# Loads and first groups in arrival order, a staged norm chain, and w_o tiles moved among the ff1 groups of a hybrid decoder block

## The chip, the cores and the metric

One Trainium2 chip, 8 cores, each with its own slice of the batch and sequence and no traffic between them. The metric is device time in microseconds of the slowest core, as the median of several executions. TensorE (PE in the profile) multiplies and transposes; VectorE (DVE), ScalarE (ACT) and GpSimd (POOL) do the elementwise work and SyncE (SP) issues loads and stores.

Some executions fall in a slow state, in which the cores of a die show a lower granted clock (in the slow run of start_only, 1174.41 us, 0.859 to 0.866 on one die against 0.965 to 0.967 on the other). The time after "Measured" is the median of all executions; those of wgp_only, start_only, staged_in_place and stage_c_last take in one slow run each, that of tr5_first two.

## The reference, cut to what matters

```python
u = rms_norm(h, mix_pre_g)
proj = u @ w_in                       # GLU (2 x 1024), pool (1024), gates (2 x 1024)
y_conv = conformer_conv_branch(...)   # GLU, depthwise conv of 31, layer norm, swish, projection
y_pool = pooling_branch(...)          # trailing means, per-group linear, projection
merged = g_conv * y_conv + g_pool * y_pool
h = h + rms_norm(merged @ w_o, mix_post_g)
v = rms_norm(h, mlp_pre_g)
v = jnp.square(jax.nn.relu(v @ w_ff1)) @ w_ff2
h = h + rms_norm(v, mlp_post_g)
```

A core has 2048 positions: 16 tiles of 128, in 4 blocks of 512. Products are in bf16, norms in float32.

## The kernel before: the parts that matter

All instructions are recorded in one order, and each engine carries out its own in that order. A helper adds the semaphore waits, so a late producer holds everything that is recorded behind its consumer on the same engine. The stages are: pool projection (`p_group`), GLU with the convolution, two gated stages, w_o with the first ff1 block, then ff2 and three more ff1/ff2 blocks.

```python
def x_norm(j):                                   # ACT square+sqrt, DVE reciprocal and scaling
    r = rstd(src, P, 0, dst, "act")
    STT(dst, src, r, gb0[:P, :], ALU.mult, ALU.mult)      # L250
def x_tr(j):                                     # 8 transposes (L223), one copy, ACT or DVE in turn
    ...
for blk in range(4):                             # projection
    if blk == 0:
        p_halo()                                 # first, and needs all of the weights
    for cc in range(8):
        nxt = 4 * (blk + 1) + cc // 2
        if cc % 2 == 0 and nxt < 16: x_norm(nxt)
        p_group(cc, blk)
        if cc % 2 == 1 and nxt < 16: x_tr(nxt)
        ...
# (cut: GLU, convolution; gated stages)
wload2(wgp, w_in_v[:, :, 4096:5120])             # after the GLU loop
def wo_tile(j):
    ...                                          # 16 matmuls
    resid(b, gb1, 2, res, dst[:, 0:512], j, "pool")   # 2 squares, add, POOL rsqrt, 4 DVE steps
    r = rstd(res, 128, 0, dst, "pool")                # square, POOL rsqrt
    STT(dst, res, r, gb2, ALU.mult, ALU.mult)         # second norm
for blk in range(4):                             # second gated stage
    for cc in range(8):
        gated(cc, blk, wco, s_t, wgc, False)
        if blk and cc % 2 == 1: wo_step()        # 12 of the 16 tiles here
        elif blk and len(trq) > 1: h_tr(trq.popleft())
# (cut: the other 4 tiles stand among the first 8 of the 32 ff1 groups of block 0)
FF1_ORDER = (0, 4, 1, 5, 2, 6, 3, 7)             # order in which ff2 takes its weight chunks
```

## Time and profile before

| | kernel before |
|---|---|
| first runs | 1085.21, 1088.69 (fast), 1103.85, 1107.53 (slow) |
| profiled span | 1084.3 us, fast, core 2 |
| PE busy | 972.8 us |
| projection ends (first GLU matmul) | 120.1 us |
| GLU stage | 154.0 |
| wait for `wgp` and first gated stage | 154.7 |
| second gated stage | 153.8 |
| ff1 of block 0, to the start of ff2 | 103.4 |
| the rest | 398.3 |

The rows from "projection ends" on add up to the span, and each is the time between two marks on PE. What a change does is looked for in the row where it acts. The lines of the profile are in the prediction.

### The profile page before, as it was taken

What the parts mean: (1) busy time and instruction counts of PE and PEld (TensorE: products, weight loads), DVE (VectorE), ACT (ScalarE), POOL (GpSimd) and SP (SyncE); (2) the same over time, 40 slices, a digit from 0 to 9 for tenths busy, and PEclk for the clock granted to TensorE, in tenths of its full rate; (3) what the DMA queues carried; (4) which work ended last, traced back from release to release, by engine and by line L of the source; (5) the groups of instructions that cost most, each with busy time, mean ns of one, the idle gap of its engine ahead of it and who ended that gap; (6) DMA issues with size and microseconds to landing.
All of it is one profiled execution on the core that took longest, in us unless ns stands there. A gap on an engine that the chain in (4) does not pass through costs nothing.

```text
span 1084.3 us, 14235 instructions; the slowest of 8 cores (1072.2 to 1084.3 us)
## 1 busy us (share of the span) xinstructions
PE 972.8 (90%) x5042; PEld 488.0 (45%) x5136; DVE 424.6 (39%) x685; ACT 311.9 (29%) x565; POOL 62.6 (6%) x112
## 2 busy tenths in 40 slices
PE   1578999999199999999999679899999999999997
PEld 1333557666054454444444334344444444444443
DVE  2276662344025412356565444124422342234222
ACT  3355213234021344133433343112321232123210
POOL 2000000100000000011211130000000000000000
PEclk9998999999689999999999979999999999999999
DMA  9922534993858002242837579522002200220021
GB/s 186 192 97 55 104 40 99 128 167 59 135 99 155 1 1 78 31 112 91 175 97 177 124 154 161 105 78 78 1 1 78 78 0 2 78 77 2 1 70 66
DMA packets 49748, 93.03 MB, mean 86 GB/s; under 512 B 6640, under 2 KB 29424, under 8 KB 48528
## 3 DMA queue, kind: packets, MB, share of 16 engines
q0 software_dynamic: 32416, 46.14, 27.8%
q1 hardware_dynamic: 17264, 45.99, 12.8%
q8 instruction: 42, 0.69, 0.3%
q14 instruction: 26, 0.21, 0.1%
HBM read 121.42 MB, written 16.84 MB: 128 GB/s over the span
## 4 chain that ended last, share of the span: by engine, by line
PE 75%; DMA 9%; DVE 6%; issue 4%; ACT 3%; POOL 1%; DVEq 0%; ACTq 0%; SPq 0%; POOLq 0%
PE ps L220 72%; DMA arena<-w_in 5%; DMA arena<-w_ff 4%; ACT arena L238 3%; PE ps L223 2%; DVE arena L250 2%; DVE arena L241 2%; DVE arena L436 1%; DVE ps L250 1%; DMA arena<-xh 1%; POOL arena L262 1%; POOL sm L370 1%; DVE ps L246 0%; DVE arena L256 0%; POOL sm L369 0%
## 5 line engine op out<-in xcount | busy, mean ns | idle before, releaser
L220 PE MATMUL ps<-arena 128*128 128x512 bf16 (+2 forms) x4514 | 941.2, 367 | 57.1 <-DMA arena<-w_in 33.8
L220 PEld LDWEIGHTS ps<-arena 128*128 128x128 bf16 x4608 | 453.8, 104 | 525.9 <-issue 81.8
L238 ACT ACTIVATE arena<-ps 128x512 bf16<-128x512 f32 (+5 forms) x382 | 237.4, 638 | 655.6 <-PE ps L220 469.5
L246 DVE TENSOR_SCALAR ps<-ps 128x512 f32<-128x512 f32 x128 | 88.2, 698 | 108.4 <-PE ps L220 108.4
L241 DVE TENSOR_TENSOR arena<-ps,arena 128x512 f32<-128x512 f32 (+3 forms) x116 | 87.0, 755 | 92.9 <-ACT arena L238 61.8
L250 DVE SCALAR_TENSOR_TENSOR arena<-arena,ps 128x512 bf16<-128x512 f32 (+1 forms) x64 | 43.9, 685 | 127.5 <-ACT arena L238 72.1
L223 PE MATMUL ps<-identb,arena 128*128 128x128 bf16 (+1 forms) x520 | 40.4, 230 | 46.4 <-DVE arena L250 29.4
L241 DVE TENSOR_TENSOR sm<-sm 128x1 f32<-128x1 f32 x32 | 5.0, 157 | 191.9 <-ACT arena L238 191.9
L223 PEld LDWEIGHTS ps<-identb,arena 128*128 128x128 bf16 (+1 forms) x520 | 34.7, 103 | 61.0 <-issue 54.5
L238 ACT ACTIVATE arena<-arena 128x1024 bf16<-128x1024 f32 (+1 forms) x33 | 34.7, 1052 | 87.7 <-DVE arena L241 87.7
L250 DVE SCALAR_TENSOR_TENSOR arena<-arena,sm 128x1024 bf16<-128x1024 f32 (+1 forms) x33 | 42.4, 1284 | 43.4 <-POOL sm L370 41.5
L250 DVE SCALAR_TENSOR_TENSOR ps<-ps,sm,arena 128x512 f32<-128x512 f32 x64 | 48.3, 754 | 21.0 <-POOL sm L370 19.4
L241 DVE TENSOR_TENSOR arena<-arena 128x512 bf16<-128x512 f32 (+2 forms) x56 | 38.4, 690 | 4.2
L560 DVE BATCH_NORM_STATS2 bnst<-arena 128x6 f32<-128x512 bf16 x32 | 20.0, 680 | 0.0
L238 ACT ACTIVATE arena<-ps,vec 128x1024 bf16<-128x1024 bf16 x16 | 19.3, 1204 | 2.5 <-PE ps L223 1.7
L262 POOL DMA_DIRECT2D arena<-w_ff x16 | 13.7, 868 | 102.2 <-PE ps L220 101.8
L374 DVE RECIPROCAL sm<-sm 128x1 f32<-128x1 f32 (+1 forms) x33 | 5.4, 162 | 34.6 <-ACT sm L238 34.6
L370 POOL TENSOR_TENSOR sm<-sm,mhalf 128x1 f32<-128x1 f32 x32 | 18.1, 567 | 4.8 <-POOL sm L369 0.2
L262 POOL DMA_DIRECT2D arena<-w_in x14 | 12.5, 920 | 87.6 <-PE ps L220 76.8
L250 DVE SCALAR_TENSOR_TENSOR arena<-arena 128x512 bf16<-128x512 f32 x24 | 16.5, 687 | 1.3
L262 POOL DMA_DIRECT2D arena<-convw x8 | 4.3, 542 | 216.0 <-PE ps L220 131.5
L369 POOL TENSOR_SCALAR sm<-sm 128x1 f32<-128x1 f32 x32 | 7.0, 220 | 151.5 <-DVE sm L241 76.2
(31 smaller groups left out, 85.8 us busy)
## 6 DMA issues: line engine op xcount, KB each, us to landing
arena<-xh SPq DMA_DIRECT2D x32, 512.0 KB, 5.3
arena<-w_ff POOLq DMA_DIRECT2D x16, 1024.0 KB, 14.1
out<-arena SPq DMA_DIRECT2D x32, 512.0 KB, 2.9
arena<-convw POOLq DMA_DIRECT2D x8, 1536.0 KB, 13.0
arena<-out SPq DMA_DIRECT2D x16, 512.0 KB, 4.1
arena<-w_in POOLq DMA_DIRECT2D x12, 512.0 KB, 19.5
arena<-w_in POOLq DMA_DIRECT2D x2, 2048.0 KB, 21.0
arena<-gb SPq DMA_DIRECT2D x5, 512.0 KB, 5.1
```

Source lines behind the costliest of these rows:

```text
L220: kb.op("pe", lambda e: e.matmul(o, lhsT=l, rhs=r, start=start, stop=stop), [l, r], [o])
L223: kb.op("pe", lambda e: e.transpose(o, i, idn), [i, idn], [o])
L238: kb.op("act", lambda e: e.activation(out=o, in_=i, func=func, **kw), rd, wr)
L241: kb.op(eng, lambda e: e.tensor_tensor(out=o, in0=a, in1=b, op=op), [a, b], [o])
L246: kb.op("dve", lambda e: e.tensor_scalar(out=o, in0=a, scalar1=s1, scalar2=s2, op0=op0, **kw), rd, [o])
L250: kb.op("dve", lambda e: e.scalar_tensor_tensor(out=o, in0=a, scalar=s, in1=b, op0=op0, op1=op1), rd, [o])
L262: return kb.op("pool", lambda e: e.dma_start(out=o, in_=src), [], [o], dma=True, after=after)
L369: kb.op("pool", lambda e: e.tensor_scalar(out=o, in0=i, scalar1=EPS[epsc], scalar2=None, op0=ALU.add), [i], [o])
L370: kb.op("pool", lambda e: e.tensor_tensor(out=o, in0=o, in1=mhalf[:, 0:n], op=ALU.pow), [o, mhalf[:, 0:n]], [o])
L374: kb.op("dve", lambda e: e.reciprocal(o, o), [o], [o])
L436: kb.op("dve", lambda e: e.tensor_tensor_scan(so, pc[:, lo:lo + n], pc[:, lo - w:lo - w + n], init, ALU.add, ALU.subtract), rd, [so])
L560: kb.op("dve", lambda e: e.bn_stats(o, i), [i], [o])
```

## The change

Its intent: let PE begin with the first x tile and the first quarter of the weights; fetch the gate weight `wgp` a stage earlier; and take the chain of squares, rsqrt, residual and second norm apart, so that several w_o tiles are under way at once. Ten of the sixteen tiles now stand between the ff1 groups.

```diff
+        LOAD(grow, gbd[0:1, :])            # one row, spread by two matmuls
+        x_load(0); x_load(1); LOAD(identf, identd) ...      # (shortened)
-        def p_group(cc, blk):
+        def p_group(cc, t0, n):            # takes a start and a width
...
+        for cc in range(2):
+            p_group(cc, 0, 256)            # half a block, as soon as x0 and x1 are there
...
+        x_tr(4)
+        x_norm(-1)                         # the halo tile
+        x_tr(5)
+        for cc in range(8):
+            p_group(cc, 512, 256)
...
+        for cc in range(8):
+            p_group(cc, 768, 256)
+            if cc % 4 == 3:
+                j = 8 + cc // 4
+                x_tr(j)
+                x_norm(j + 2)
+                pool_pump(1)
+        # block 2 begins with x_tr(10), x_norm(12), x_tr(11), x_norm(13)
...
             if q == 2:
                 weff_scale()
+                WLOAD(wgp, w_in_v[:, :, 4096:5120])
-        wload2(wgp, w_in_v[:, :, 4096:5120])
...
+            due.append(deque([stage_b, stage_c, stage_d]))   # residual; second norm; transposes
+        def tick():                        # oldest tile first
+            for d in list(due):
+                d.popleft()()
...
-                if blk and cc % 2 == 1:
-                    wo_step()
+                tick()
+                if (blk == 2 and cc % 2 == 1) or (blk == 3 and cc % 4 == 1):
+                    wo_tile(pend.popleft())
...
+                if blk == 0 and i % 2 == 1:
+                    tick()
+                    if pend:
+                        wo_tile(pend.popleft())
+                    if i in (19, 23):
+                        for n in ((6, 7) if i == 19 else (4, 5)):
+                            ff2_load(n)
+                    if i == 27:
+                        LOAD(gb3, gbd[3:4, :].partition_broadcast(128))
```

More of the change, by code (lines that the diff above doesn't have):

```diff
@@ L295, in build_program @@
         identf = av(RZ, 128, dt=F32)
+        grow = av(RZ + 256, 1024, dt=F32)[0:1, :]
+        onesr = av(RZ + 2304, 128, dt=F32)[0:1, :]
         UT = [av(TP + b * 2080, 16, 130) for b in range(2)]
@@ L343, in x_load @@
             P, r0 = (32, 0) if j < 0 else (128, H + 128 * j)
-            xev[j] = LOAD(xst[i % 4][:P, :], xh[r0:r0 + P, :])
+            xev[j] = LOAD(xst[i % 4][:P, :], xh[r0:r0 + P, :], after=[wev[2]] if j == 4 else [])
         x_order = [0, 1, 2, 3, -1] + list(range(4, 16))
-        LOAD(vec[:], vecs)
-        LOAD(gb0, gbd[0:1, :].partition_broadcast(128))
-        for j in x_order[:4]:
+        LOAD(grow, gbd[0:1, :])
+        x_load(0)
+        x_load(1)
+        LOAD(identf, identd)
+        for j in (2, 3):
             x_load(j)
+        wev = []
         for i in range(4):
-            WLOAD(w_p[:, :, i * 256:(i + 1) * 256], w_in_v[:, :, 2048 + i * 256:2048 + (i + 1) * 256],
-                  after=[xev[0]] if i == 0 else [])
-        LOAD(identf, identd)
+            wev.append(WLOAD(w_p[:, :, i * 256:(i + 1) * 256], w_in_v[:, :, 2048 + i * 256:2048 + (i + 1) * 256],
+                             after=[xev[1]] if i == 0 else []))
         for i in range(3):
@@ L357, in build_program @@
         kb.op("dve", lambda e: e.memset(mhalf[:], -0.5), [], [mhalf[:]])
+        kb.op("dve", lambda e: e.memset(onesr, 1.0), [], [onesr])
+        ACT(sm[:, 0:1], epst[:, 0:1], AF.Sqrt)
+        for hh in range(2):
+            MM(ps[:, hh, :], onesr, grow[:, hh * 512:(hh + 1) * 512], True, True)
+            COPY("dve", gb0[:, hh * 512:(hh + 1) * 512], ps[:, hh, :])
         COPY("dve", identb[:], identf)
@@ L402, in build_program @@
         bgd = deque()
+        pools = {cc: deque() for cc in (0, 7, 1, 2, 3, 6, 5, 4)}
         def pump(n):
@@ L407, in pump, with pool_pump @@
                     bgd.popleft()()
-        s2i = {"i": 0}
+        def pool_pump(n):
+            for _ in range(n):
+                for d in pools.values():
+                    if d:
+                        d.popleft()()
+                        break
         def pool_task(cc, blk):
@@ L454, in build_program @@
             kb.op("dve", lambda e, cc=cc: e.memset(p_t[:, cc, 0:16], 0.0), [], [p_t[:, cc, 0:16]])
-        def p_group(cc, blk):
+        def p_group(cc, t0, n):
             b = banks(1)
             for k in range(8):
-                MM(ps[:, b, :], w_p[:, k, cc * 128:(cc + 1) * 128], uT[:, k, H + blk * 512:H + (blk + 1) * 512], k == 0, k == 7)
-            COPY("act", p_t[:, cc, 32 + blk * 512:32 + (blk + 1) * 512], ps[:, b, :])
-            bgd.append(lambda: pool_task(cc, blk))
+                MM(ps[:, b, 0:n], w_p[:, k, cc * 128:(cc + 1) * 128], uT[:, k, H + t0:H + t0 + n], k == 0, k == 7)
+            COPY("act", p_t[:, cc, 32 + t0:32 + t0 + n], ps[:, b, 0:n])
         def p_halo():
@@ L468, in p_halo @@
             COPY("act", p_t[:, :, 16:32], ps[:, b, 0:128].rearrange("p (c t) -> p c t", c=8))
-        prev = None
-        for j in x_order[:5]:
-            x_norm(j)
-            if prev is not None:
-                x_tr(prev)
-            prev = j
-        x_tr(prev)
         def wg_load(q):
             for h2 in range(2):
-                WLOAD(wg[q % 2][:, :, h2, :], w_in_v[:, :, h2 * 1024 + q * 256:h2 * 1024 + (q + 1) * 256])
-        wg_load(0)
-        wg_load(1)
-        for blk in range(4):
-            if blk == 0:
-                p_halo()
+                WLOAD(wg[q % 2][:, :, h2, :], w_in_v[:, :, h2 * 1024 + q * 256:h2 * 1024 + (q + 1) * 256],
+                      after=[xev[13 + 2 * q]] if q < 2 else [])
@@ new lines, in build_program @@
+        x_norm(0)
+        x_norm(1)
+        x_tr(0)
+        x_norm(2)
+        x_tr(1)
+        x_norm(3)
+        for cc in range(2):
+            p_group(cc, 0, 256)
+        x_tr(2)
+        x_tr(3)
+        LOAD(vec[:], vecs)
+        for cc in range(2):
+            p_group(cc, 256, 256)
+        x_norm(4)
+        for cc in range(2, 8):
+            p_group(cc, 0, 512)
+            if cc == 4:
+                x_norm(5)
+        x_tr(4)
[3 more added lines that the diff above has]
+            p_group(cc, 512, 256)
+            if cc == 1:
+                x_tr(-1)
+                x_norm(6)
+                p_halo()
+                for c2 in range(8):
+                    pools[c2].append(lambda c2=c2: pool_task(c2, 0))
+                x_norm(7)
+            if cc == 5:
+                x_tr(6)
+                x_norm(8)
+                pool_pump(1)
@@ L487, in build_program @@
+        x_tr(7)
+        x_norm(9)
+        for cc in range(8):
+            p_group(cc, 768, 256)
+            pools[cc].append(lambda cc=cc: pool_task(cc, 1))
+            if cc % 4 == 3:
+                j = 8 + cc // 4
+                x_tr(j)
+                x_norm(j + 2)
+                pool_pump(1)
+        for blk in range(2, 4):
+            if blk == 2:
+                x_tr(10)
+                x_norm(12)
+                x_tr(11)
+                x_norm(13)
             for cc in range(8):
@@ L488, in build_program @@
                 nxt = 4 * (blk + 1) + cc // 2
-                if cc % 2 == 0 and nxt < 16:
-                    x_norm(nxt)
-                p_group(cc, blk)
+                if cc % 2 == 0 and nxt + 2 < 16:
+                    x_norm(nxt + 2)
+                if blk == 2 and cc in (1, 3):
+                    wg_load(cc // 2)
+                p_group(cc, blk * 512, 512)
+                pools[cc].append(lambda cc=cc, blk=blk: pool_task(cc, blk))
                 if cc % 2 == 1 and nxt < 16:
@@ L494, in build_program @@
                 if cc % 2 == 1 or blk == 3:
-                    pump(1)
+                    pool_pump(1)
         def conv_load(cc):
@@ L601, in build_program @@
                 glu_pair(q, rp)
+                pool_pump(1)
                 pump(3)
@@ L608, in build_program @@
                 wg_load(q + 2)
-            if q == 0:
-                pump(len(bgd))
             if q == 1:
+                pool_pump(32)
                 weff_prep()
@@ L693, in build_program, with x_reload, resid_a @@
         outh = {}
-        def resid(b, gb_t, epsc, res, junk, j, eng):
+        def x_reload(j):
+            LOAD(xr[j % 3], xh[H + 128 * j:H + 128 * (j + 1), :])
+        def resid_a(b, epsc, junk, eng):
             ac = []
             for hh in range(2):
-                a, r = col()
+                a = col()[0]
                 ACT(junk, ps[:, b + hh, :], AF.Square, scale=1.0 / 32, accum=a)
@@ L703, in resid, with resid_b @@
             rsqrt(r, ac[0], epsc, eng)
+            return r
+        def resid_b(b, gb_t, r, res, j):
             for hh in range(2):
@@ L708, in resid @@
             outh[j] = kb.op("sp", lambda e: e.dma_start(out=out[128 * j:128 * (j + 1), :], in_=res), [res], [("outh", j)], dma=True)
-        def x_reload(j):
-            LOAD(xr[j % 3], xh[H + 128 * j:H + 128 * (j + 1), :])
+        due = deque()
+        live = set()
         def wo_tile(j):
@@ L718, in wo_tile, with stage_b, stage_c, stage_d @@
             res, dst = xr[j % 3], xb2[j % 2]
-            resid(b, gb1, 2, res, dst[:, 0:512], j, "pool")
-            r = rstd(res, 128, 0, dst, "pool")
-            STT(dst, res, r, gb2, ALU.mult, ALU.mult)
-            if j + 3 < 16:
-                x_reload(j + 3)
+            junk = xb2[[i for i in (j % 2, 1 - j % 2) if i not in live][0]]
+            r = resid_a(b, 2, junk[:, 0:512], "pool")
+            v = {}
+            def stage_b():
+                resid_b(b, gb1, r, res, j)
+                v["r"] = rstd(res, 128, 0, dst, "pool")
+            def stage_c():
+                STT(dst, res, v["r"], gb2, ALU.mult, ALU.mult)
+                live.add(j % 2)
+                if j + 3 < 16:
+                    x_reload(j + 3)
+            def stage_d():
+                h_tr(j)
+                live.discard(j % 2)
+            due.append(deque([stage_b, stage_c, stage_d]))
+        def tick():
+            for d in list(due):
+                d.popleft()()
+            while due and not due[0]:
+                due.popleft()
         def h_tr(j):
@@ L740, in build_program @@
         pend = deque()
-        def wo_step():
-            if pend:
-                j = pend.popleft()
-                wo_tile(j)
-                trq.append(j)
-            if wq:
-                wq.popleft()()
-        trq = deque()
-        wq = deque()
         for blk in range(4):
@@ L755, in build_program @@
                 gated(cc, blk, wco, s_t, wgc, False)
-                if blk and cc % 2 == 1:
-                    wo_step()
-                elif blk and len(trq) > 1:
-                    h_tr(trq.popleft())
+                tick()
+                if (blk == 2 and cc % 2 == 1) or (blk == 3 and cc % 4 == 1):
+                    wo_tile(pend.popleft())
             pend.extend(range(4 * blk, 4 * blk + 4))
-            for c in (blk, blk + 4):
-                wq.append(lambda c=c: ff1_load(c))
-            if blk == 0:
-                wq.popleft()()
-                wq.popleft()()
-            if blk == 3:
-                for i in (2, 3, 0, 1):
-                    wq.append(lambda i=i: ff2_load(i))
+            ff1_load(blk)
+            ff1_load(blk + 4)
+        for i in (2, 3, 0, 1):
+            ff2_load(i)
         def ff1_group(i, blk):
@@ L787, in ff2_tile @@
                     MM(ps[:, b + hh, :], h1(i)[:, tl * 128:(tl + 1) * 128], ff2(f)[:, hh * 512:(hh + 1) * 512], i == 0, i == 31)
-            resid(b, gb3, 0, res, hT[j // 4][:, 0, :], j, "act")
+            resid_b(b, gb3, resid_a(b, 0, hT[j // 4][:, 0, :], "act"), res, j)
         for blk in range(4):
@@ L792, in build_program @@
                 ff1_group(i, blk)
-                if blk == 0 and i < 8:
-                    if i % 2 == 1:
-                        wo_step()
-                    elif len(trq) > 1:
-                        h_tr(trq.popleft())
-                    if i == 7:
-                        for s in (4, 5, 6, 7):
-                            wq.append(lambda s=s: ff2_load(s))
-                if blk == 0 and i >= 8 and wq:
-                    wq.popleft()()
-                if blk == 0 and i >= 10 and trq:
-                    h_tr(trq.popleft())
-                if blk == 0 and i == 12:
-                    LOAD(gb3, gbd[3:4, :].partition_broadcast(128))
+                if blk == 0 and i % 2 == 1:
[7 more added lines that the diff above has]
+                        LOAD(gb3, gbd[3:4, :].partition_broadcast(128))
             for tl in range(4):
```

## The prediction

> **What bounds the kernel now.** I read the cores view first: spans 1072.2 to 1084.3 us at clocks of 0.969 to 0.977, both dies alike, so the profiled run is of the fast state (1085.2 us; the runs of 1103.9 and 1107.5 are over 1.5% above it and count as slow). Then the page: PE busy 90%, DVE 39%, ACT 29%. Then the two rows by slices:
>
> ```profile
> PE   1578999999199999999999679899999999999997
> PEclk9998999999689999999999979999999999999999
> ```
>
> A slice is 27.1 us. TensorE is full except at the start (slices 0 to 3), in slice 10 and in slices 22 to 24, and the granted clock dips after the holes. From 700 us to the tail it is dense. So the kernel is bound by TensorE's amount of work, plus about 111 us in which it waits (1084.3 - 972.8), plus matmuls at a lower clock after waits. PE's waits (us in total, times, longest):
>
> ```profile
> PE ps L220 <- DMA arena<-w_in: 33.8, 3, 25.6
> PE ps L223 <- DVE arena L250: 29.4, 16, 5.5
> PE ps L223 <- DVE sm L374: 17.0, 1, 17.0
> PE ps L220 <- ACT arena L238: 9.5, 9, 2.1
> PE ps L220 <- DMA arena<-w_ff: 4.0, 2, 3.7
> ```
>
> L220 is a matmul, L223 a transpose, L250 the scaling by the norm. The timeline places them. The start, and the hole in slice 10 with the issue that ends it:
>
> ```profile
> 10.77 1.28 ACT L238 ACT_TABLE_LOAD   x1 [10.77 <-DMA arena<-xh]
> 15.04 0.23 DVE L256 CAST identb<-arena 128x128 bf16<-128x128 f32 x1 [13.74 <-DMA arena<-ident]
> 16.96 1.01 PE L223 MATMUL ps<-identb,arena 128*128 128x128 bf16 x8 [16.96 <-DVE sm L374]
> 38.40 0.57 PE L220 MATMUL ps<-arena 128*128 128x16 bf16 x16 [5.47 <-DMA arena<-w_in]
> ```
>
> ```profile
> 272.94 0.53 POOL L262 DMA_DIRECT2D arena<-convw  x1 [20.59 <-PE ps L220]
> 273.63 0.90 POOL L262 DMA_DIRECT2D arena<-w_in  x1 [0.17 <-issue]
> ```
>
> ```profile
> 299.71 3.57 PE L220 MATMUL ps<-arena 128*128 128x512 bf16 x8 [25.58 <-DMA arena<-w_in]
> ```
>
> The transposes wait for the late identity, the first projection groups for all four chunks of weights (the halo group, which comes first, needs all of them), and at 273.6 the 2 MB gate weight `wgp` is issued only when it is needed: on its in-order queue it stands behind the last convolution weight, which waits for a buffer. In the w_o stage:
>
> ```profile
> 609.05 0.91 PE L223 MATMUL ps<-identb,arena 128*128 128x128 bf16 x8 [3.48 <-DVE arena L250]
> 621.57 0.61 PE L223 MATMUL ps<-identb,arena 128*128 128x128 bf16 x8 [3.05 <-DVE arena L250]
> ```
>
> ```profile
> 600.00:620.00 20.00, 14.03 (x61) 5.97 (x61) 8.43 (x13) 6.01 (x13) 4.10 (x9) 0.91 0.57 134
> 620.00:640.00 20.00, 15.63 (x67) 7.08 (x69) 8.66 (x13) 7.67 (x16) 4.15 (x8) 0.83 0.71 120
> 640.00:660.00 20.00, 14.46 (x66) 6.58 (x65) 10.06 (x15) 8.25 (x13) 6.02 (x9) 0.83 0.92 175
> ```
>
> (After the length: busy PE, weight load, DVE, ACT, POOL; clock, DMA share, GB/s.) One tile goes round in 12.5 us (609.05 to 621.57) while no engine is full: squares, POOL's rsqrt, residual, second norm and transposes stand in one chain, and only two ff1 groups lie beside it.
>
> **What the Trainium skill says.** "TensorE: Matmul & The Clock Gate", Part 1, has TensorE at half clock after an idle window of some 3.4 us and for as long at the restart. The trace agrees: 446 ns per matmul (3.57/8) after the 25.58 us hole, against 219 ns in the dense part (10.74 us for 49). So a removed hole brings its clock loss back too. "DMA: Bandwidth & Descriptors", Queues, rings and completion order, says that each DMA engine takes a ring's descriptors in order; the trace's landings agree: the 512 KB broadcast of `gb0` at 7.96 us, then x0 10.70, x1 12.02, x2 13.51, x3 14.73, identity 14.94. Its section "Issuing engines are not separate DMA queues" has the issuers share the engines; the weight chunks land at 19.90, 25.05, 32.22 and 38.26 with x tiles in between, and core 1's second, little disturbed, comes 3.2 us after its first. "ScalarE: Activation LUTs", What ACT_TABLE_LOAD costs, gives 1283 ns; the trace has 1.28 us at 10.77.
>
> **Part by part.**
>
> *Start and projection.* `gb0` comes as one row, spread by two matmuls and two copies. Its landing came 4.5 us after that of the load before it (3.49), so x0 should land near 6 us, x1 7.3, identity 8, x3 10.5; a dummy Sqrt takes the table load away. Weights now wait for x1: issue at 7.5, and with before's latency of 8.6 the first chunk lands near 16. x4 is held until chunk 2 and the GLU weights until x13, so chunks 1 and 2 follow at 3.2 us (19, 22), chunk 3, beside x4 to x6, near 29. PE then works in that order: two half groups (16 matmuls, cold, 213 ns, half of the 425 that full ones stand apart near 40 us: 3.4 us) to 19.4; transposes, copy and the other halves to 24; groups 2 to 7 at 1.75 us each (8 x 219 ns) to 34.5. Before, block 0 ran from 39.2 to 58. For block 1 I count 14.7 us of half groups (128 x 115 ns; the 128-column convolution matmuls run at 65 ns each, so 256 columns are not bound by weight loads), halo 2.1, transposes 2.5, waits of some 4 for norms and copies: 59. Blocks 2 and 3: 28 us of groups, 3.5 of transposes, 2.5 of waits: 93. Before: block 3 began at 104.43, its first 12 matmuls took 4.22 us, 52 more at 219 ns: 120. Gain 27. The extra cost is small: 160 half matmuls at about +6 ns, and evictions.
>
> *Pool tasks one per GLU pair instead of three.* Takes away the 2.4 us wait for DVE at 151.9 and the cold 12 matmuls behind it (4.54 against 2.63 us). In a pair PE has 3.5 us (16 x 219 ns) against DVE's 2.8 (0.69 and a task of 2.1). Gain 4.
>
> *`wgp` issued a stage earlier.* It now stands ahead of the last two convolution weights; its buffer is free after the pool weights are scaled, about 40 us before use, against 13 us of transfer (it and `w_conv_out` landed 10.3 us apart, the first 13.1 after the convolution weight ahead). Gain 25.6 plus clock: granted 0.86 over 300 to 320, that is 2.8. Gain 28.
>
> *w_o.* From the last gated group (582.6) to ff2 (686.0) before took 103.4 us for 32 ff1 groups (56.1), 5 w_o tiles (17.5) and 6 sets of transposes (0.54 each, 3.2): 76.9. So 26.5 are waits and clock. After, 10 tiles stand here, one per two ff1 groups, so the five moved in (20 us) lie outside the balance. PE has 3.5 + 3.5 + 0.54 = 7.55 us per tile and the chain three such periods. But ACT and DVE work in order, and a loop appears: squares 1.55, add and rsqrt or two relus 1.5, residual 3.1 (601.91 to 605.00), rstd square 1.35, transposed copy 0.95: some 8.5 us with hops. That is 1 us per tile over PE's period; over nine intervals 9, less 1.5 of slack in banks: I charge 7. Gain 19.5. In gated block 3 the transposes of tiles 4 and 5 come three groups (10.5 us) behind their tile, the chain takes 12: +1.5.
>
> *ff2 weights.* Slots 6, 7, 4, 5 come only after the last w_o tile, 12 groups and 3 transposes (23 us) before ff2. They landed 6.2 us apart before, the first about 10 after issue: the fourth 31 to 36 us after the tile. PE waits 4 to 8 us, against 4.0 before: +2.
>
> Sum: -27 - 4 - 28 - 19.5 + 1.5 + 2 = -75, span 1009, time some 1.6 more (1085.9 against 1084.3): 1011.
>
> **Rivals.** (1) ACT and DVE bind the projection: with x0 to x3 ready PE goes at its rate, but ACT has per tile 2.0 us of norm and copy and up to 1.5 of evictions (3.5 of PE's 4.1), so norms come late, as in the 16 waits for L250. For it: order on ACT puts the square of x4 before six evictions. Against: norms now run two tiles ahead, and fewer pool tasks stand between. It would take 10 us of the 27: 1021. (2) The loop of DVE and ACT is worse than I charge, or the ff2 wait grows: 1020. (3) Half groups hide everything and the loop is absorbed by eight banks: 998. (4) A denser TensorE draws the die into the slow state more often: 1028 to 1032, against 1104 before. (5) `wgp` hides but the displaced convolution weight 7 becomes the wait: it lands 13 us after its issue and is needed some 20 us after: unlikely, +3.
>
> **Range and chances.** 1012, for a fast run; 994 holds rival 3 with luck, 1032 rivals 1 and 2 together or a median of slow runs. Even with half of the gain the time falls 3.5%; within 2% needs two of three big gains to vanish.
>
> **What would show it.** In the changed profile: no wait of 20 us on w_in and a full slice 10; the first p matmul near 16 us, first GLU near 93; gaps of 1 us at ff1 groups released by DVE or ACT instead of 3 to 5 us at transposes, clock 1.0 there; waits on w_ff of 4 to 8 us. I am wrong if the projection ends after 105, if a weight still holds PE before the gated stage, or if the w_o stage keeps waits over 3 us.

## The result, and the profile after

The changed kernel took 1045.24 us (median of 4, 1044.92 to 1046.79). Ratios are the mean time of one kernel's fast runs over that of the other's fast runs of the same rounds, so not quite the ratio of the medians: here 0.9619, 95% interval 0.9588 to 0.9650. It is faster, as foretold, but 33 us slower than the predicted 1012 and outside the range.

| us | before | after | predicted after |
|---|---|---|---|
| projection ends | 120.1 | 106.1 | 93 |
| GLU stage | 154.0 | 150.1 | 150 |
| `wgp` wait and first gated stage | 154.7 | 126.3 | 126.7 |
| second gated stage (with 11 tiles up to its end before, 6 after) | 153.8 | 138.1 | 135 |
| first ff1 block (with 5 tiles before, 10 after) | 103.4 | 113.7 | 104 |
| the rest | 398.3 | 410.7 | 400 |

(The predicted column carries the terms of the sum to the stages; the five tiles that moved past the mark take 20 us from the fourth row to the fifth.) Four rows miss: 13, 3, 10 and 10 us, together 36.

The rows of the changed kernel's page, by slices of 26.1 us:

```profile
PE   5779999999999999999888885999999999999996
PEclk9889999999999999999999997999999999999999
```

The start and slice 10 are as the prediction had them. New are the eights of slices 19 to 23 and the 5 in slice 24. PE's waits in the changed kernel (us in total, times, longest):

```profile
PE ps L223 <- DVE arena L250: 13.0, 6, 4.0
PE ps L220 <- DMA arena<-w_ff: 12.0, 2, 10.7
PE ps L220 <- DVE arena L241: 11.0, 9, 2.0
PE ps L220 <- DMA arena<-w_in: 4.2, 1, 4.2
```

The 33.8 us for `w_in` are down to 4.2, and between 250 and 310 us PE waits for nothing. But L241, a DVE addition, is new on this list, and `w_ff` has tripled. PE's timeline of the projection:

```profile
17.63 3.57 PE L220 MATMUL ps<-arena 128*128 128x256 bf16 x16 [4.22 <-DMA arena<-w_in]
...
41.84 3.57 PE L220 MATMUL ps<-arena 128*128 128x256 bf16 x16 [3.94 <-DVE arena L256]
...
69.23 1.01 PE L223 MATMUL ps<-identb,arena 128*128 128x128 bf16 x8 [4.00 <-DVE arena L250]
...
72.52 5.97 PE L220 MATMUL ps<-arena 128*128 128x512 bf16 x15 [2.27 <-ACT arena L238]
```

The number in brackets is the wait just before, with what ended it. The first p matmul (17.63 against "near 16") and the end of block 0 (35.95 against 34.5) are nearly as predicted. Then come three waits of 2 to 4 us, each with cold matmuls behind, that is, matmuls at a lower granted clock: 16 half-width ones in 3.57 us at 41.84, 15 full ones in 5.97 us at 72.52 (398 ns each, against 219). Why there, DVE's timeline shows, first for tile 5's copy, then for tiles 11 and 10:

```profile
39.82 1.27 DVE L250 SCALAR_TENSOR_TENSOR arena<-arena,sm 32x1024 bf16<-32x1024 f32 x1 [0.42 <-DVE sm L383]
41.02 0.67 DVE L256 COPY arena<-ps 128x1024 bf16<-128x1024 bf16 x1
```

```profile
67.70 1.28 DVE L250 SCALAR_TENSOR_TENSOR arena<-arena,sm 128x1024 bf16<-128x1024 f32 x1
68.90 1.25 DVE L452 TENSOR_TENSOR_SCAN arena<-arena 128x528 f32<-128x528 f32 x1
...
71.30 0.69 DVE L256 COPY arena<-ps 128x1024 bf16<-128x1024 bf16 x1
```

At 39.82 DVE scales the halo tile (the 32 rows ahead of the core's own), whose rows come late from ACT; the copy that the next p groups wait for was recorded behind it. At 67.70 it scales tile 11, between whose norm and transposes no p group is recorded; then a pool task (the scan and what belongs to it) stands before the copy of tile 10.

The ff1 stage in PE's timeline, one w_o tile per line, and the busy times of 20 us of it (columns as in the prediction):

```profile
592.00 3.61 PE L220 MATMUL ps<-arena 128*128 128x512 bf16 x16 [1.08 <-DVE arena L241]
...
600.60 3.61 PE L220 MATMUL ps<-arena 128*128 128x512 bf16 x15 [1.08 <-DVE arena L241]
```

```profile
580.00:600.00 20.00, 16.56 (x87) 7.53 (x86) 12.79 (x20) 10.94 (x21) 3.15 (x8) 1.00 0.55 173
```

The chain's waits of up to 5.5 us per tile at the transposes are gone from this stretch and the clock is 1.00, but the period, the time from one tile to the next, is 8.60 us, where PE's own work is 7.55. DVE and ACT in one period:

```profile
552.96 1.27 DVE L250 SCALAR_TENSOR_TENSOR arena<-arena,sm 128x1024 bf16<-128x1024 f32 x1
554.16 0.75 DVE L250 SCALAR_TENSOR_TENSOR ps<-ps,sm,arena 128x512 f32<-128x512 f32 x1
...
557.38 1.06 ACT L238 ACTIVATE arena<-arena 128x1024 bf16<-128x1024 f32 x1 [2.72 <-DVE arena L241]
```

The second norm of the tile before (1.27 us at 552.96) stands ahead of the residual step of the next (from 554.16). ACT is idle for 2.72 us until that residual is done (557.38). Last, the start of ff2:

```profile
645.72 3.57 PE L220 MATMUL ps<-arena 128*128 128x512 bf16 x8 [10.67 <-DMA arena<-w_ff]
650.65 39.63 PE L220 MATMUL ps<-arena 128*128 128x512 bf16 x171 [1.36 <-DMA arena<-w_ff]
```

12.03 us of waiting against 4.0 before, and 8 cold matmuls. In the trace the chunks for slots 6 and 7 are issued at 614.9 and land at 629.0 and 639.3; those for 4 and 5 are issued at 628.5 and land at 645.6 and 650.5. (A slot is the memory of one 1 MB chunk.) ff2 needs slot 4 after only four matmuls. Slot 4 lies where the last w_o tile has its residual x: its load goes out 0.8 us after the store of that residual has landed (issued at 619.2, landed at 627.65). The same 0.8 us stand in the traces of all twelve kernels with the staged chain.

### The profile page after: what moved, and what is told of

It is laid out like the page before. It is cut to its first block, busy times and chain, and to the rows that moved or that the text cites. A ratio compares the mean times of both kernels' runs of the same rounds, so it can differ in the third digit from the quotient of the medians.

```text
span 1044.9 us, 14360 instructions; the slowest of 8 cores (1039.9 to 1044.9 us)
## 1 busy us (share of the span) xinstructions
PE 971.9 (93%) x5129; PEld 497.0 (48%) x5220; DVE 424.3 (41%) x688; ACT 316.1 (30%) x576; POOL 62.4 (6%) x112
## 4 chain that ended last, share of the span: by engine, by line
PE 78%; DMA 9%; DVE 5%; issue 3%; ACT 3%; POOL 0%; DVEq 0%; SPq 0%; ACTq 0%; POOLq 0%
PE ps L220 76%; DMA out<-arena 4%; ACT arena L238 3%; DMA arena<-w_ff 2%; PE ps L223 2%; DMA arena<-xh 2%; DVE arena L241 2%; DMA arena<-w_in 1%; DVE arena L250 1%; DVE ps L250 1%; POOL arena L262 0%; DVE ps L246 0%; DVE arena L452 0%; DVEq L159 0%; SPq L259 0%
## 5 line engine op out<-in xcount | busy, mean ns | idle before, releaser
L220 PE MATMUL ps<-arena 128*128 128x512 bf16 (+4 forms) x4601 | 942.5, 363 | 47.4 <-DMA arena<-w_ff 12.0
L220 PEld LDWEIGHTS ps<-arena 128*128 128x128 bf16 (+1 forms) x4692 | 463.2, 104 | 509.0 <-issue 65.4
L238 ACT ACTIVATE arena<-ps 128x512 bf16<-128x512 f32 (+6 forms) x392 | 241.0, 625 | 645.3 <-PE ps L220 473.6
L241 DVE TENSOR_TENSOR arena<-ps,arena 128x512 f32<-128x512 f32 (+3 forms) x116 | 86.9, 754 | 73.0 <-ACT arena L238 44.7
L250 DVE SCALAR_TENSOR_TENSOR arena<-arena,ps 128x512 bf16<-128x512 f32 (+1 forms) x64 | 43.9, 686 | 145.5 <-ACT arena L238 117.7
L241 DVE TENSOR_TENSOR sm<-sm 128x1 f32<-128x1 f32 x32 | 5.1, 158 | 223.3 <-ACT arena L238 223.3
L223 PE MATMUL ps<-identb,arena 128*128 128x128 bf16 (+1 forms) x520 | 38.9, 227 | 17.6 <-DVE arena L250 13.0
L250 DVE SCALAR_TENSOR_TENSOR ps<-ps,sm,arena 128x512 f32<-128x512 f32 x64 | 48.1, 752 | 1.9 <-DVE sm L383 0.4
L250 DVE SCALAR_TENSOR_TENSOR arena<-arena,sm 128x1024 bf16<-128x1024 f32 (+1 forms) x33 | 42.2, 1280 | 3.5 <-POOL sm L379 1.4
L241 DVE TENSOR_TENSOR arena<-arena 128x512 bf16<-128x512 f32 (+2 forms) x56 | 38.3, 690 | 5.8 <-ACT arena L238 1.6
L452 DVE TENSOR_TENSOR_SCAN arena<-arena,scr 128x512 f32<-128x512 f32 x12 | 15.3, 1276 | 4.8 <-ACT arena L238 4.8
L250 DVE SCALAR_TENSOR_TENSOR arena<-arena 128x512 bf16<-128x512 f32 x24 | 16.5, 687 | 1.2
```

Source lines behind the costliest of these rows:

```text
L220: kb.op("pe", lambda e: e.matmul(o, lhsT=l, rhs=r, start=start, stop=stop), [l, r], [o])
L223: kb.op("pe", lambda e: e.transpose(o, i, idn), [i, idn], [o])
L238: kb.op("act", lambda e: e.activation(out=o, in_=i, func=func, **kw), rd, wr)
L241: kb.op(eng, lambda e: e.tensor_tensor(out=o, in0=a, in1=b, op=op), [a, b], [o])
L250: kb.op("dve", lambda e: e.scalar_tensor_tensor(out=o, in0=a, scalar=s, in1=b, op0=op0, op1=op1), rd, [o])
L452: kb.op("dve", lambda e: e.tensor_tensor_scan(so, pc[:, lo:lo + n], pc[:, lo - w:lo - w + n], init, ALU.add, ALU.subtract), rd, [so])
```

## The experiments

Thirteen kernels ran; all gave correct results. The kernel before, run beside them, had medians of 1086.6 to 1088.9 us. "Gained against the changed kernel" is the difference of the two ratios times 1087 us. The 0.9619 comes from an earlier round, with two fast runs of the kernel before; its interval alone is 3.4 us either way, so that a gain under some 4 us is not clear of noise by the times alone. (gb3_early, with one load moved, came to 0.9612 in a later round.)

### The parts of the change one by one

**wgp_only**: the kernel before, with only the load of `wgp` moved.

```diff
             if q == 2:
                 weff_scale()
+                WLOAD(wgp, w_in_v[:, :, 4096:5120])
-        wload2(wgp, w_in_v[:, :, 4096:5120])
```

> The kernel before with one thing alone: the gate weight wgp issued after the third GLU quarter instead of after the fourth. Theory (this part did what was predicted): the 25.6 us wait and about 2.8 us of lower clock behind it vanish and nothing takes their place: 28 us less, ratio 0.974, and the first gated matmul follows the last GLU matmul without a wait. Rival (the loads queued behind it come late): a wait on convw or on w_conv_out of 5 us or more appears afterwards, gain 20 us or less, ratio 0.982 or more.

Measured: 1060.17 us, ratio 0.9742 (0.9722 to 0.9762), so -28 us, give or take 2, as expected.

**start_only**: the kernel before, with the new start, projection order and pool tasks (the hunks up to the GLU loop), without the others.

> The kernel before with the new start, half groups and pool tasks alone. Theory (the account of the two profiles): the projection ends at about 106 us instead of 120 and the GLU stage is 4 us shorter, so 18 us less, ratio 0.983; the waits of 4 us at the transposes of tile 11 and at the first half groups of block 1 are there as in the changed kernel. Rival (the start is worth the predicted 27 and 4 us, and only beside the other parts it loses some): 31 us less, ratio 0.971.

Measured: 1070.04 us, ratio 0.9841 (0.9821 to 0.9861), so -17.3 us, where the prediction had -31 for these hunks. The two waits are there (3.96 and 4.09 us in its trace). The loss is there with the w_o part absent: it belongs to the projection.

**wo_only**: the staged chain and the moved tiles alone (the hunks from `x_reload` on).

> The kernel before with the staged w_o chain and the moved tiles alone. Theory (the move gives back what the staging wins): the second gated stage and the first ff1 block together 5 us shorter, the first ff2 tile 8 us of w_ff wait and 2 to 4 of lower clock longer: total +7 us, ratio 1.006, between 1.00 and 1.01. Rival (as the prediction had it): 16 us less, ratio 0.985.

Measured: 1089.08 us, ratio 1.0013 (0.9997 to 1.0029). The size +7 was missed, but it is in the stated range: the part for which the prediction had -16 (-19.5, +1.5, +2) gains nothing. The three parts alone add up to -44, the whole change to about -41: within the noise they do not interact.

**staged_in_place**: the staged chain in the kernel before, with the tiles at their old places, so that the loads of the ff2 weights come earlier as well. The edit, against wo_only:

```diff
-                if (blk == 2 and cc % 2 == 1) or (blk == 3 and cc % 4 == 1):
+                if blk and cc % 2 == 1:
                     wo_tile(pend.popleft())
-                    if i in (19, 23):
-                        for n in ((6, 7) if i == 19 else (4, 5)):
+                    if i in (7, 11):
+                        for n in ((6, 7) if i == 7 else (4, 5)):
-                    if i == 27:
+                    if i == 13:
                         LOAD(gb3, ...)
```

> The kernel before with the staged chain, but the w_o tiles at their old places (12 among gated groups, 4 among ff1 groups), ff2 weights issued as soon as their slots are free. Theory (the place of the tiles costs, not the staging): waits in the ff1 block fall from 17.6 us to some 8, their clock loss of 8.6 goes, the wait on w_ff stays at 5 or less: 18 us less than before, ratio 0.983, and at least 20 us less than wo_only. Rival (the staged order itself makes the waits, as DVE and ACT work in order): within 5 us of wo_only.

Measured: 1070.94 us, ratio 0.9849 (0.9835 to 0.9864): 16 us under the kernel before, 18 under wo_only, where at least 20 was expected. The waits for the ff2 weights and for L241, first of wo_only, then of this kernel:

```profile
PE ps L220 <- DMA arena<-w_ff: 12.1, 2, 10.7
PE ps L220 <- DVE arena L241: 11.9, 9, 2.4
```

```profile
PE ps L220 <- DVE arena L241: 6.7, 4, 2.4
PE ps L220 <- DMA arena<-w_ff: 5.8, 2, 4.4
```

The ff2 wait, 5.8 us, is a little over the 5 expected. Staging the chain gains 16 us; moving the tiles, with the loads that depend on them, gives it back.

**after_in_place**: the same edit in the whole changed kernel.

> The changed kernel with the w_o tiles put back to their old places (12 among gated groups, 4 among ff1 groups), the staged chain kept. Theory (the place costs, and independently of the other parts): 18 us less than the changed kernel, as staged_in_place stood 17.8 below wo_only: ratio to before 0.9455, PE waits in the first ff1 block under 10 us in all and 6 or less on w_ff. Rival (with the earlier parts in place the tiles among gated groups meet a busier DVE or DMA): ratio 0.955 or more, new waits in the second gated stage.

Measured: 1028.42 us, ratio 0.9457 (0.9435 to 0.9478): 17.6 us gained. Among the gated groups (384 to 557 us) PE waits for nothing in its trace; the ff2 wait is 7.8 us, over the 6 expected. So half of the miss hangs on where the tiles stand, with the loads that come earlier for it.

### The loop of the ff1 stage

**copy_dve**: my first theory was that the transposed copy on ACT, which I had counted in the loop, sets the 8.60 us.

```diff
-            COPY("act", hT[j // 4]...
+            COPY("dve", hT[j // 4]...
```

> The changed kernel with one instruction per tile moved: the copy of the transposed tile goes from ACT to DVE. Theory (the pace of 8.60 us per tile is the loop squares, add, relus, residual, rstd square, copy, and DVE has idle time at the add): without the copy's 0.95 us in the loop the period is 7.6 to 7.8 us, PE's own, the waits of about 1.1 us at the ff1 groups nearly vanish, 8 to 10 us less than the changed kernel, ratio 0.953. Rival A (DVE is simply too full in this stage): the period grows by up to 0.7 us, ratio 0.964 or more. Rival B (x tiles that land late set the pace): the period stays at 8.6, ratio 0.960 to 0.964.

Measured: 1053.77 us, ratio 0.9687 (0.9670 to 0.9704): slower than the changed kernel. The theory fell; rival A had the numbers. PE's timeline of this run:

```profile
596.91 3.61 PE L220 MATMUL ps<-arena 128*128 128x512 bf16 x16 [1.74 <-DVE arena L241]
...
606.16 3.61 PE L220 MATMUL ps<-arena 128*128 128x512 bf16 x16 [1.74 <-DVE arena L241]
```

The period is 9.25 us, 0.65 more, which is the 0.68 us of one copy on DVE. So DVE carries the loop, and ACT's copy lies in ACT's idle time. Adding up the changed kernel's own lines from 551.65 to 560.25 gives it whole: add 0.11, two relus 1.20, the second norm of the tile before 1.20, residual 3.07 and a hop of 0.15, square and read-out 1.29, two squares of the next tile 1.58, together 8.6. The second norm is in the loop only because `tick` records the oldest tile first.

**stage_c_last**: the same steps, with the second norm recorded after the residual step.

```diff
-            for d in list(due):
-                d.popleft()()
+            steps = [d.popleft() for d in list(due)]
+            for f in sorted(steps, key=lambda f: f.__name__ == "stage_c"):
+                f()
```

> The changed kernel with one edit: when several chain steps fall due between two groups, the second norm (stage c) is recorded last instead of first, so on VectorE the residual step of the next tile no longer stands behind it. Theory (the 1.27 us of the second norm is inside the loop that feeds the first ff1 block): the steady period falls from 8.60 us to 7.5-7.8 (TensorE's own work), the waits of about 1.1 us for the two relus (L241) nearly vanish in the ff1 stage, and the kernel gains 6-9 us against the changed one: ratio to the kernel before 0.952-0.956. Rival (VectorE's total work per tile binds, so that the order does not matter): period 8.5 or more, ratio 0.960 or more.

Measured: 1037.02 us, ratio 0.9536 (0.9515 to 0.9557), 9 us gained. PE's timeline, then DVE's and ACT's:

```profile
589.91 7.19 PE L220 MATMUL ps<-arena 128*128 128x512 bf16 x32
...
597.38 7.18 PE L220 MATMUL ps<-arena 128*128 128x512 bf16 x32
```

```profile
594.72 1.28 DVE L250 SCALAR_TENSOR_TENSOR arena<-arena,sm 128x1024 bf16<-128x1024 f32 x1
594.95 1.06 ACT L238 ACTIVATE arena<-arena 128x1024 bf16<-128x1024 f32 x1 [1.59 <-DVE arena L241]
```

The period is 7.47 us (589.91 to 597.38), with no wait: PE's own work. The second norm (594.72) now runs beside ACT's square (594.95). PE's waits for L241 fell from 11.0 to 2.0 us in all. The rival, that DVE's amount of work binds, falls, and with it the reason that rival A gave above: the amount is the same.

### The order in the projection

**tr5_first**: tile 5's transposes before the halo's norm.

```diff
         x_tr(4)
-        x_norm(-1)
         x_tr(5)
+        x_norm(-1)
```

> The changed kernel with two lines swapped before block 1 of the projection: the transposes of x tile 5 are recorded before the norm of the halo tile. Theory (the copy of tile 5 stands on DVE behind the halo's scaling, which waits for ACT): the 3.9 us wait of the first half group of block 1 falls under 1.5 and its cold matmuls partly go: 3 to 6 us less than the changed kernel, ratio 0.9565 to 0.959. Rival (ACT's work as a whole sets the pace of the projection, an order only moves the wait): under 1.5 us less, ratio 0.9605 or more, a longer wait at the halo transposes or at tile 6.

Measured: 1044.06 us, ratio 0.9586 (0.9563 to 0.9608), 3.6 us gained, near the lower edge of what the theory expected. By the times alone that is not clear of noise, and the interval reaches the rival's 0.9605; in its trace block 3 of the projection starts 2.1 us earlier (89.93 against 92.04). PE's timeline:

```profile
38.13 1.01 PE L223 MATMUL ps<-identb,arena 128*128 128x128 bf16 x8 [2.27 <-DVE arena L250]
...
40.08 3.57 PE L220 MATMUL ps<-arena 128*128 128x256 bf16 x16 [0.94 <-DVE arena L256]
```

The 3.94 us are down to 0.94, but tile 5's transposes waited 2.27 here (0.73 in the changed kernel), and the groups behind are still cold. One wait went and a smaller one showed, which is in part what the rival had said.

**norm11_early**: tile 11's norm recorded three groups earlier, and without the second pool task beside it.

```diff
                 x_tr(j)
-                x_norm(j + 2)
-                pool_pump(1)
+                if j == 8:
+                    x_norm(10)
+                    pool_pump(1)
+            if cc == 4:
+                x_norm(11)
```

> The changed kernel with the norm of x tile 11 recorded three half groups earlier in block 1, and without the pool task at the end of that block. Theory (the norm stands right before its own transposes, so its whole chain lies open, and the pool task's scan holds up the copy): the 4.0 us wait at the transposes of tile 11 and the 2.3 us after it fall under 2 together, and the cold matmuls behind them go: 5 to 9 us less than the changed kernel, ratio 0.954 to 0.9575. Rival (ACT's work sets the pace): under 2 us less, ratio 0.960 or more.

Measured: 1040.46 us, ratio 0.9566 (0.9549 to 0.9583), 5.8 us gained. The waits of 4.00 and 2.27 us are 1.04 and 1.61, together over the 2 expected, and the matmuls behind are still slow (16 in 5.30 us). Which of the two edits won it, the earlier norm or the dropped pool task, was not separated:

```profile
68.40 0.61 PE L223 MATMUL ps<-identb,arena 128*128 128x128 bf16 x8 [1.04 <-DVE arena L250]
70.62 5.30 PE L220 MATMUL ps<-arena 128*128 128x512 bf16 x16 [1.61 <-ACT arena L238]
```

### The ff2 weights

**gb3_early**: the load of `gb3` (512 KB, 12.7 us to land while the chunks were under way) moved from ff1 group 27 to group 1.

```diff
-                    if i == 27:
+                    if i == 1:
                         LOAD(gb3, ...)
```

> The changed kernel with the load of block 3's gated values issued at the second ff1 group of the stage instead of the 28th, so that it no longer shares the engines with the four ff2 weight chunks. Theory (contention lengthens the landings): the wait for the ff2 weights falls from 12.0 us to about 8 (6 to 9), the chunks land 5-7 us apart, 3-5 us gained against the changed kernel, ratio 0.957-0.960. Rival (when the slots come free and the order in the queue set the wait alone): wait stays 11-13 us, ratio 0.961-0.963.

Measured: 1044.20 us, ratio 0.9612 (0.9594 to 0.9631). The wait came to 10.4 us, a little under the rival's 11 to 13 and above the theory's 6 to 9, and the time is the rival's. The first two chunks landed 7.1 us apart instead of 10.3, but the last came 20.1 us after the second pair was issued (22.1 in the changed kernel). Sharing the engines with `gb3` accounts for 1.6 of the 12.0 us at most. That leaves when the second pair is issued, which no run here changed alone, and its place in the queue against the order of need, which the next run tests.

**ff2_parts**: ff2 takes the six chunks that land first for both halves of the output, then slots 4 and 5 (the edit does so in every tile; it matters in the first).

```diff
-            for hh in range(2):
-                for i in range(32):
+            for part in ((0, 2, 4, 6, 5, 7), (1, 3)):
+                for hh in range(2):
+                    for p in part:
+                        for i in range(4 * p, 4 * p + 4):
```

> The changed kernel with each ff2 contraction of the first tile taken in two parts: the chunks that land early (slots 0, 2, 4, 6 and 5, 7 of the list, which leaves the two that are queued last to the end) for both halves, then the last two. It moves the first need of the late chunks from about 1 us to about 10 us after the start of ff2. Theory (the wait is the order of need against the order of the queue): the wait for the ff2 weights falls from 12.0 us to 2-5, 7-9 us gained with the clock, ratio 0.953-0.956. Rival (the early chunks land no sooner than needed, so the wait only moves to them): wait 8 us or more, ratio 0.958 or more.

Measured: 1037.99 us, ratio 0.9549 (0.9531 to 0.9568), 7.6 us gained. The wait fell from 12.0 to 6.0 us, more than the 2 to 5 expected, since the last chunk (650.5) lands later than the moved need:

```profile
650.60 39.77 PE L220 MATMUL ps<-arena 128*128 128x512 bf16 x174 [3.90 <-DMA arena<-w_ff]
```

### All together

**best**: the mends of tr5_first, norm11_early, stage_c_last and ff2_parts, and the tiles in their old places.

> All of the mends at once: the changed kernel with the moved w_o tiles back in their old places, the halo order and the early norm of tile 11 in the projection, the second norm last, ff2 in two parts. Theory (the parts that were measured add: 1028 with the tiles in place, less 3 and 5 in the projection, less 4 to 8 for the loop and ff2): 1008-1016 us, ratio 0.927-0.935. Rival (the mends overlap, since with the tiles in place the loop has slack and the weights come early): 1018-1022 us, ratio 0.936-0.940.

Measured: 1009.47 us (median of 4), ratio 0.9287 (0.9267 to 0.9307), 18.5 us under after_in_place. Faster than both kernels. PE's row of its page, by slices of 25.2 us:

```profile
PE   4889999999999999999999799999999999999996
```

Between the start and the tail only slice 22 falls below 8; one wait of 5.31 us for a second norm (L250, at 573.96) lies in it.

**four_mends**: the same four mends with the tiles where the change put them. It asks whether the four causes are separate.

> The changed kernel with the four mends of order alone (tile 5's transposes ahead of the halo's norm, tile 11's norm earlier, the second norm last among the chain steps, ff2 in two parts), the w_o tiles left where the change put them. Theory (these four causes are separate, so that what each gave alone adds up: 3.6, 5.8, 9.0 and 7.6 us, worked out from the ratios 0.9586, 0.9549 and so on against 0.9619, 26 us in all): 1018-1023 us, ratio 0.936-0.940, most of the 33 us by which the prediction missed. Rival (they overlap: what one removes, another wait takes): 1026 us or more, ratio 0.943 or more. What is left over the predicted 1012 then lies in the gated stage's tiles 4 and 5 and in the rest of the projection's waits.

Measured: 1020.02 us (median of 5, 1019.77 to 1021.03), ratio 0.9382 (0.9362 to 0.9401). The gain is 25.8 us against 26.0 summed from the single runs. The sum takes the 0.9619 four times, so that an agreement this close is luck, but the rival's 1026 is ruled out: no overlap shows. Block 3 of the projection starts 9.1 us earlier than in the changed kernel (82.95 against 92.04), as the two mends there should give together. PE's wait at ff2 in this run is 4.08 us:

```profile
631.61 18.71 PE L220 MATMUL ps<-arena 128*128 128x512 bf16 x72 [4.08 <-DMA arena<-w_ff]
```

Of the predicted 1012, 8 us are left. The projection here ends near 97 (block 3 starts at 82.95, and its 64 matmuls at 219 ns take 14), 4 later than predicted. In the rest of the kernel up to ff2 there are still three waits for L250, 8.7 us in all, of which the changed kernel had two of the same length (2.77 and 3.28 us, at the transposes of tiles 4 and 5, where 1.5 was charged); the third, at the last tile, was 1.81 us there and is 2.60 here.

## Why the prediction was wrong, by its own steps

**The start: right.** First matmul, weight chunks (17.28, 21.23, 24.89 and 29.60 in the trace, against 16, 19, 22 and 29) and block 0 came within 3 us.

**The rest of the projection: wrong by 13 us, and past the end of 105 that I had named as the sign.** The failing step is "norms now run two tiles ahead". That is so within blocks 2 and 3, but I did not follow the recorded order across the seams: tile 11's norm has no p group between it and its transposes, and tile 5's copy is behind the halo's scaling on DVE. I had charged "waits of some 4" for block 1 and 2.5 for blocks 2 and 3; the three waits at 41.84, 69.23 and 72.52 alone are 10.2 us, with the clock loss behind them. (Two slips of mine changed nothing: my terms for block 1 add up to 57.8, not 59, and the low slices of the w_o stage are 22, 23 and 25.) Mending the two orders won 3.6 and 5.8 us. Some 4 us are left, in waits of 0.6 to 1.9 us that I did not take apart.

**GLU and pool tasks, `wgp`: right.** 150.1 against 150, and -28.4 against -28, confirmed alone by wgp_only. The rival that a convolution weight becomes the wait did not come.

**The loop of the ff1 stage: the mechanism right, the members wrong.** I had foreseen a loop of ACT and DVE of "some 8.5 us" and the period is 8.60, but for the wrong reason: the transposed copy that I counted is not in it, and the second norm, which I left out, is. I also took 1.5 us of slack off, and charged nothing for periods of 9.4 to 9.5 us where a reloaded x tile came late. (Its load goes out only when the store out of the same buffer has landed: 562.99 after 562.82.) The stage took 113.7 us against 104. For L241, the loop, PE waited 10.4 us in it where 7 was charged, and 5.1 us more at the transposes of tile 5 and of the last tile, with matmuls at half clock behind tile 5's. For tiles 4 and 5 together I had charged 1.5 us; they waited 2.77 and 3.28, and the second is also over the 3 us that I had named as a sign of being wrong. Recording the second norm last wins 9 us; the other waits were not isolated.

**The ff2 weights: wrong by 10 us.** The term of +2 took before's landings (first about 10 us after issue, then every 6.2). After, the first landed 14.1 us after its issue and the second 10.3 us later; the second pair was issued only at 628.5 and landed 17 and 21 us after its issue. It was not the last tile's second norm that held it (done at 622.96) but the store of that tile's residual out of slot 4's memory: 8.5 us to land, with the first pair and `gb3` under way, where the store of the tile before took 2.6. The prediction did not count that store; a run with another buffer for that tile would show what the 5.5 us are worth. I also missed that the change queues 6 and 7 before 4 and 5, while the order of need has 4 second and 5 fourth. ff2_parts shows the order of need to be worth 7.6 us; gb3_early puts the share of `gb3` at 1.6 us of wait or less.

**Moved tiles as neutral: wrong.** I let the moved tiles "lie outside the balance". But among ff1 groups a tile comes with 7.55 us of PE work, less than the loop's 8.60, while in the old places the transposes of one tile follow those of the last by 11.1 us (502.23 and 513.33 in best), more than the loop; and the buffers of the ff2 weights come free later. Put back, the same chain gains about 18 us, in two different kernels.

The rivals had the right places, and both came, larger than charged: (1) had 10 us for the projection, where it was 13, and (2) had 9 for the loop or the ff2 wait, where both grew, by 20 together. The reason that (1) gave first, that ACT has too much work per tile, is not what the runs show: a change of order, with one pool task put off, won most of it back. How much of after_in_place's 17.6 is the loop and how much the earlier loads is not separated by these runs; best against four_mends puts what is left of the move, with both mended, at 10.3 us (0.9382 less 0.9287).

## What to carry to other kernels

Ask of every producer where it is recorded in its engine's own order, seam by seam, and not how many tiles ahead it is on average: one instruction off the path, placed before one on it, cost here 1.1 us in every period. When work is moved to shorten a chain, look at what its end releases: here the last w_o tile, and the store of its residual, free the buffers of the next weights, so moving it later gave back all that the better chain had won. And let the order of use follow the order of arrival.

## What the Trainium skill lacked or had wrong

- "TensorE: Matmul & The Clock Gate", Part 1, has half clock follow an idle window of some 3.4 us. Here shorter waits were enough: after 2.77 us (at 504.62 in the changed kernel) and 2.27 us (tr5_first) the eight transposes were cold at once, 1.01 us. Nor did the length of the wait tell it: the same 2.77 us in four_mends (495.52) left the clock at 1.00, and after 3.28 us (527.30 in the changed kernel) the transposes took 0.61 us and the clock fell to 0.50 only behind them, from 528.5 to 531.0. The same part lets its windows run free of the kernel, which may be why; no run here tests it.
- "DMA: Bandwidth & Descriptors", Bandwidth, gives 6.15 us for a 1 MB load, a single-core number. With eight cores at it, the first of a pair of 1 MB weight loads landed 14.1 us after its issue, in the changed kernel and in four_mends, and the second 23.6 and 23.4 us after its own; the page has no figure for a pair with other loads and a store of the same core under way.
- No page looked at tells how the place of an off-path instruction on an in-order engine lengthens a loop: 1.27 us of DVE work recorded first or last made the period 8.60 or 7.47 us.
